# Layer 1's banded attention with TensorE's order written out by hand

## The chip, the cores and the metric
The kernel runs on one core of one Trainium2 chip. The metric is the device time of one launch in microseconds (us); lower is better.

## The reference
A two-layer encoder over one sequence of 2048 tokens of width 1024, in float32. Layer 0 mixes a dilated and a differential attention. Layer 1, which the change touches, is banded grouped-query attention: 16 query heads of 64, four to each of 4 key/value heads, each token attending to the 128 tokens on either side, with a learned sink per head:

```python
proj = h @ w_in                                   # odd_mixer; h is the normalised, modulated x
q, k, v, g = jnp.split(proj, [MIX_WIDTH, MIX_WIDTH + C_KV_WIDTH, MIX_WIDTH + 2 * C_KV_WIDTH], axis=-1)
...
m, l, acc = banded_attention(q, k, v, slopes, 1, C_HALF_WINDOW)
sk = sink.astype(jnp.float32).reshape(C_KV_HEADS, R)[None, :, :, None]
M = jnp.maximum(m, sk)
e = jnp.exp(m - M)
y = acc * e[..., None] / (l * e + jnp.exp(sk - M))[..., None]
y = y.transpose(0, 3, 1, 2, 4).reshape(B, S, MIX_WIDTH).astype(h.dtype)
return (y * jax.nn.silu(g)) @ w_out
```

## The kernel before
Tokens lie in 16 tiles of 128 and 4 blocks of 512 (TB = 4). TensorE is PE here, VectorE DVE, ScalarE ACT, GpSimd POOL; SP issues nearly all DMAs. Each float32 product is made of three matmuls on split operands (`three`, L292: high x high, high x low, low x high), so a 512-column step over one of 8 slices of the width is 3 matmuls, and a projection piece (128 columns of the weights for one block) is 24.

Layer 1 for a block b needs its normalised and transposed h (`layer1_norm`, eight tiles `pt_h` of four transposes, split into `h1T` by ACT, POOL and DVE), then `layer1_qkv`: two key pieces, one value piece (`pn`, 256 columns, weights `wh`/`wl`), eight query pieces. `layer1_gate` has eight gate pieces for a block. In `proj_pieces` the raw weights `wr` are loaded, ACT makes the high half of `wt` (L340), and DVE (even pieces) or POOL (odd pieces) the low half (L341); for the value piece POOL makes both low halves (L355). `wt`, `wh` and `wl` share two buffers. h of blocks 0, 1 and 2 is stored to `hD1` (L1068) and read again as `h1G` (L1090) for the gates.

`attend` (L1114) treats one tile t, for which keys and values of tiles t-1 to t+1 are loaded, and goes through four groups kv of four heads. A head's scores are `pqC` (L586, L587); DVE adds the distance table and takes the row maximum (L1146) into `sC` and `mxC`; one DVE multiply per group makes `nmC` (L1151); ACT takes the exponential (L1154). For each key tile u the four heads' scores are transposed into `ptC` (L1160), split into `hC` and `lC` (for u = t by ACT and POOL, else by ACT and DVE; L1166 to L1171) and multiplied with the values into `pyC` (L1173). The denominators of all 16 heads are made on DVE and ACT (L1184 to L1188), transposed on PE (`pd`, L1190), copied (`dtC`), stored to memory (`fC`, L1193), read back twice with broadcast (L1196), and POOL multiplies `yC` with them (L1198).

In the loop over blocks, attention of the tiles whose keys are there goes along with the projections of the next block, by a `tick` after each group; with block 3 go the gates of blocks 3, 0 and 1, and those of block 2 follow after attention, tied behind its last score. That is the order in which the code is written; the order on every engine is set by a scheduler that simulates the program (`schedule_with_timeline_sim=True`), so instructions may run elsewhere than where they are written. Each engine's queue is then fixed.

Of the kernel before, what the change touches and what calls it, by code (L numbers as in the profile page):

```python
# [11 lines left out]
F32 = mybir.dt.float32  # L12
# [9 lines left out]
P = 128  # L22
# [59 lines left out]
def tile_encoder(ctx: ExitStack, tc: tile.TileContext, x, c, ada_w, ada_b, norm_g, ab_w_in, ab_w_out,  # L82
# [7 lines left out]
    def scratch(name, shape, dt=F32):  # L90
        return dram.tile(shape, dt, name=name, tag=name)
# [9 lines left out]
    hD = scratch("hD", [TB, 2, P, KC * 512])  # L101
    hD1 = scratch("hD1", [TB - 1, 2, P, KC, 512])
    fB = scratch("fB", [B_H, S], F32)
# [227 lines left out]
    def proj_pieces(pool, ps, w, h, b, pieces, name, after=lambda b, n: None):  # L331
# [3 lines left out]
        for n, (c0, sink_T, sink_N) in enumerate(pieces):  # L335
            if sink_T is not None:
# [6 lines left out]
                for k in range(KC):  # L343
                    three(pt, (wt[:, 0, k], wt[:, 1, k]), (h[0][k], h[1][k]), k, KC, None if k else after(b, n))
                sink_T(pt, b)
                yield
            else:
# [8 lines left out]
                for j in range(4):  # L356
                    pt = ps.tile([P, 512], F32, name=f"pn_{name}_{b}_{n}_{j}", tag="mm")
                    cols = slice(j * P, (j + 1) * P)
                    for k in range(KC):
                        three(pt[:, :CH], (h[0][k][:, cols], h[1][k][:, cols]), (hi[:, k], lo[:, k]), k, KC)  # L360
                    sink_N(pt[:, :CH], 4 * b + j)
                    yield
# [328 lines left out]
    def dilated_attention(pool, poolc, ps_, fill, psf):  # L691
# [49 lines left out]
        def tick():  # L741
            steps[0] += 1
            if steps[0] % 2 == 0:
                next(gate, None)

# [308 lines left out]

    def layer1_norm(pool, ps, b):
# [7 lines left out]
        h = [[pool.tile([P, 512], FR, name=f"h1T{b}_{i}_{k}", tag="hk", bufs=20) for k in range(KC)] for i in range(2)]  # L1063
        norm_block(pool, ps, 1, b, xs, h)
        if b < TB - 1:
            for k in range(KC):
                for i in range(2):
                    nc.sync.dma_start(hD1[b, i, :, k], f32(h[i][k]))  # L1068
        return h

# [13 lines left out]
    def layer1_gate(pool, ps, h, b, after=lambda b, n: None):  # L1084
        if h is None:
            h = [[pool.tile([P, 512], FR, name=f"h1G{b}_{i}_{k}", tag="hk", bufs=20) for k in range(KC)]
                 for i in range(2)]
            for k in range(KC):
                for i in range(2):
                    nc.sync.dma_start(f32(h[i][k]), hD1[b, i, :, k])  # L1090
# [22 lines left out]

    def attend(pool, ps, t, V, consts, tick):  # L1114
        tab, nsl, isl, sk = consts
        u0, u1 = max(t - 1, 0), min(t + 2, NT)
        n, o = (u1 - u0) * P, (u0 - t + 1) * P
        for u in range(u0, u1):
# [13 lines left out]
        for a in range(2):  # L1132
            nc.sync.dma_start(f32(Q)[a * 64:(a + 1) * 64],
                              qC[t // 4][a, :, :, t % 4 * P:(t % 4 + 1) * P].rearrange("h f s -> f h s"))
# [4 lines left out]
        for kv in range(C_KV):  # L1139
            Sx = []  # L1140
            for r in range(4):
                h = 4 * kv + r
                pq = ps.tile([P, 384], F32, name=f"pqC{t}_{h}", tag="s")
                last = scores(pq[:, :n], Q[:, h], KH[:, kv, :n], Q[:, h], KL[:, kv, :n])
                s_ = pool.tile([P, 384], F32, name=f"sC{t}_{h}", tag="p", bufs=8)
                nc.vector.tensor_tensor_reduce(out=s_[:, :n], in0=pq[:, :n], in1=tab[:, o:o + n], scale=1.0,  # L1146
                                               scalar=isl[:, h:h + 1], op0=OP.add, op1=OP.max,
                                               accum_out=mx[:, h:h + 1])
                Sx.append(s_)
            hs = slice(4 * kv, 4 * kv + 4)  # L1150
            nc.vector.tensor_tensor(nm[:, hs], mx[:, hs], nsl[:, hs], op=OP.mult)  # L1151
            for r in range(4):
                h = 4 * kv + r
                nc.scalar.activation(Sx[r][:, :n], Sx[r][:, :n], AF.Exp, bias=nm[:, h:h + 1], scale=slope_C(h),  # L1154
                                     accum_out=ls[:, h:h + 1])
            py = ps.tile([P, 512], F32, name=f"pyC{t}_{kv}", tag="y")
            for u in range(u0, u1):
                pt = ps.tile([P, 512], F32, name=f"ptC{t}_{kv}_{u}", tag="t")
# [13 lines left out]
                for i, w in enumerate((hi, lo)):  # L1172
                    nc.tensor.matmul(py, V[u][:, kv], w, start=(u == u0 and i == 0), stop=(u == u1 - 1 and i == 1))  # L1173
            tmp = pool.tile([P, 512], F32, name=f"hsC{t}_{kv}", tag="hs", bufs=2)
            nc.scalar.activation(tmp[64:], py[64:], AF.Copy)
            for a in range(2):
                nc.vector.tensor_tensor(
                    y[a * 64:(a + 1) * 64, 2 * kv:2 * kv + 2],
                    tmp[64:].rearrange("p (g a q) -> p a g q", a=2, q=P)[:, a],
                    py[:64].rearrange("p (g a q) -> p a g q", a=2, q=P)[:, a], op=OP.add)  # L1180
            tick()

        d = sm.tile([P, C_H], F32, name=f"dC{t}", tag="dC", bufs=2)
        nc.vector.tensor_tensor(d, sk, nm, op=OP.add)  # L1184
        nc.scalar.activation(d, d, AF.Exp)
        nc.vector.tensor_tensor(d, d, ls, op=OP.add)
        nc.vector.tensor_scalar(d, d, 2.0, None, op0=OP.mult)
        nc.vector.reciprocal(d, d)  # L1188
        pd = ps.tile([P, 512], F32, name=f"pd{t}", tag="y")
        nc.tensor.transpose(pd[:C_H, :P], d, ident)  # L1190
        dt = sm.tile([C_H, P], F32, name=f"dtC{t}", tag="dtC", bufs=2)
        nc.scalar.activation(dt, pd[:C_H, :P], AF.Copy)
        nc.sync.dma_start(fC[t], dt)  # L1193
        F = pool.tile([P, KC, P], F32, name=f"fC_{t}", tag="f", bufs=1)
        for a in range(2):
            nc.sync.dma_start(F[a * 64:(a + 1) * 64].rearrange("p k q -> p (k q)"),  # L1196
                              fC[t].rearrange("(k a) q -> a k q", a=2)[a:a + 1].to_broadcast([64, KC, P]))
        nc.gpsimd.tensor_tensor(y, y, F, op=OP.mult)  # L1198
        nc.sync.dma_start(yC[t], y)
        return last  # L1200

# [12 lines left out]
    with sbuf("pO") as pool_:  # L1214
# [8 lines left out]
        with sbuf("pO2") as pool2, psum("psO") as ps_:  # L1223
# [9 lines left out]
            layer0_out(pool, Bufs(ps_, o=5), w, [upper, lower], g, x, x1d, "0", "o", range(FULL))  # L1233
            h1 = layer1_norm(pj, psj, 0)
            for _ in layer1_qkv(pj, psj, h1, 0, qs):
# [5 lines left out]
    with sbuf("pC") as pool, psum("psC") as ps_:  # L1241
        ps = Bufs(ps_, s=2, t=2, y=2)
        consts = layer1_consts(pool)
        V = {}
        for b in range(TB):
            ts = range(max(4 * b - 1, 0), 4 * b + 3 if b < TB - 1 else NT)

            if b + 1 < TB:
                h1 = layer1_norm(pj, psj, b + 1)
                between, n = layer1_qkv(pj, psj, h1, b + 1, qs), 14  # L1250
            else:
                between, n = chain(*(layer1_gate(pj, psj, h1 if g == TB - 1 else None, g)
                                     for g in (TB - 1, *range(TB - 2)))), 8 * (TB - 1)
            at = [0, 0]

            def tick():
                at[0] += 1
                while at[1] * len(ts) * C_KV < at[0] * n:
                    at[1] += 1
                    next(between, None)  # L1260

            for t in ts:
                last = attend(pool, ps, t, V, consts, tick)
            for _ in between:
# [42 lines left out]
```

## Time and profile before

| | |
|---|---|
| median of 3 runs | 3063.69 us (3059.81 to 3064.14) |
| the profiled execution, its span | 3054.52 us, 3052.5 us |
| mean granted TensorE clock | 0.964 |
| layer 0's last matmul starts | 2119.14 us |
| layer 1's last attention product starts | 2821.51 us |

Times in the profile count from the start of the span. The durations of matmuls overlap, since they are pipelined; the pace of PE is read from their starts. A wait is put down to the instruction whose result came last.

### The profile page before, as it was taken

The page shows a single profiled execution, that of the slowest core. Times are in us where ns is not written, and L with a number is a line of the kernel's source. Part 1 is how long each engine was busy: PE and PEld are TensorE (multiplying, and loading weights), DVE is VectorE, ACT ScalarE, POOL GpSimd, SP SyncE. Part 2 cuts the span into 40 slices and gives each one's busy share as a digit, 9 for nine tenths or more (in the row PEclk, how much of TensorE's full clock was granted, in tenths as well). Part 3 has the DMA queues.
Part 4 walks back from the last instruction along what each step waited for, and adds up shares of the span by engine and source line. Part 5 has one row for each costly group of instructions (what it writes and reads, how often), then busy time and mean ns, then how long its engine had stood idle before and what let it go on. Part 6 is the DMA issues. An engine that isn't in the chain of part 4 may idle for free. (4 is left out here: it accounts for less than half of the span.)

```text
span 3052.5 us, 43787 instructions
## 1 busy us (share of the span) xinstructions
PE 2797.3 (92%) x15056; PEld 2351.4 (77%) x15056; DVE 1894.7 (62%) x4120; ACT 1491.3 (49%) x2841; POOL 1147.5 (38%) x755
## 2 busy tenths in 40 slices
PE   6999899999999998899888887999889999999997
PEld 5788788878888887677776666787778788877786
DVE  7425286777677678755556767454465765556576
ACT  5311255556555555555556762223465765656321
POOL 3200075555655644322424333332334443333221
PEclk9999899999999999999999998999999999999999
DMA  6687743653655551298786888685988778885754
GB/s 264 228 289 232 208 139 109 190 176 121 165 157 161 153 167 42 64 273 238 201 238 172 203 226 246 222 295 198 246 205 223 188 179 205 228 214 154 219 187 155
DMA packets 554552, 593.78 MB, mean 195 GB/s; under 512 B 32257, under 2 KB 421594, under 8 KB 548186
## 3 DMA queue, kind: packets, MB, share of 16 engines
q1 hardware_dynamic: 542490, 574.21, 65.6%
q10 hardware_dynamic: 11840, 16.78, 1.6%
q8 instruction: 119, 1.95, 0.3%
q14 instruction: 103, 0.84, 0.1%
HBM read 414.36 MB, written 176.46 MB: 194 GB/s over the span
## 5 line engine op out<-in xcount | busy, mean ns | idle before, releaser
L637 ACT ACTIVATE s<-s,nm 128x2048 f32<-128x2048 f32 x128 | 256.7, 2006 | 140.5 <-DVE nm L636 140.4
L643 POOL TENSOR_SCALAR s<-s,rr 128x1536 f32<-128x1536 f32 x64 | 122.7, 1916 | 342.3 <-DVE rr L641 237.7
L586 PE MATMUL pq<-kB,q 128*128 128x512 f32 x512 | 217.5, 425 | 29.5 <-DVE mx L631 16.5
L646 POOL TENSOR_TENSOR s<-s,s 128x1536 f32<-128x1536 f32 x64 | 231.7, 3620 | 4.9
L658 ACT ACTIVATE th<-pt 128x512 fp32r<-128x512 f32 x256 | 147.1, 594 | 174.6 <-PE pt L654 132.3
L1146 DVE CUSTOM_DVE_ANT_0 sC<-pqC,tabC,isl 128x384 f32<-128x384 f32 (+1 forms) x256 | 147.5, 597 | 125.0 <-PE pqC L587 73.9
L587 PE MATMUL pq<-kB,q 128*128 128x512 f32 x512 | 206.7, 404 | 0.0
L631 DVE CUSTOM_DVE_ANT_0 s<-pq,ndist 128x1024 f32<-128x1024 f32 x128 | 156.0, 1218 | 78.1 <-PE pq L587 56.0
L659 DVE TENSOR_TENSOR tl<-pt,th 128x512 fp32r<-128x512 f32 x256 | 170.4, 683 | 51.0 <-ACT th L658 50.7
L631 DVE CUSTOM_DVE_ANT_0 s<-pq,ndist,mx 128x1024 f32<-128x1024 f32 x128 | 163.5, 1277 | 28.5 <-PE pq L587 26.0
L1154 ACT ACTIVATE sC<-sC,nmC 128x384 f32<-128x384 f32 (+1 forms) x256 | 151.0, 593 | 39.8 <-DVE nmC L1151 39.5
L297 PE MATMUL py<-tl,vB 128*128 128x256 f32 x512 | 152.4, 298 | 14.7 <-DVE tl L659 13.8
L654 PE MATMUL pt<-ident,s 128*128 128x128 f32 x1024 | 153.1, 277 | 2.7 <-DVE s L644 2.2
L294 PE MATMUL py<-th,vB 128*128 128x256 f32 x512 | 150.2, 293 | 2.4 <-ACT th L658 2.3
L586 PEld LDWEIGHTS pq<-kB,q 128*128 128x128 f32 x512 | 98.9, 193 | 62.9 <-DVE mx L631 26.0
L298 PE MATMUL py<-th,vB 128*128 128x256 f32 x512 | 146.3, 286 | 0.0
L341 POOL TENSOR_TENSOR wt_g<-wr_g,wt_g 128x1024 fp32r<-128x1024 f32 x32 | 77.1, 2408 | 182.8 <-ACT wt_g L340 177.5
L989 POOL TENSOR_TENSOR yr<-yr,gr 128x512 f32<-128x512 f32 (+1 forms) x46 | 62.5, 1360 | 209.5 <-DMA yr<-yC 37.2
L1167 POOL TENSOR_SCALAR hC<-rC 128x512 fp32r<-128x512 f32 x64 | 42.6, 666 | 255.9 <-ACT rC L1166 220.0
L1160 PE MATMUL ptC<-ident,sC 128*128 128x128 f32 x736 | 134.0, 282 | 3.1 <-ACT sC L1154 2.6
L294 PE MATMUL pp_l<-h1T,wt_l 128*128 128x512 f32 x320 | 129.0, 404 | 7.3 <-ACT wt_l L340 6.8
L298 PE MATMUL pp_l<-h1T,wt_l 128*128 128x512 f32 x320 | 129.0, 405 | 5.4 <-POOL wt_l L341 3.4
(417 smaller groups left out, 9181.7 us busy)
## 6 DMA issues: line engine op xcount, KB each, us to landing
wr_a<-in_ab_w_in_dram SPq DMA_DIRECT2D x48, 512.0 KB
wr_l<-in_c_w_in_dram SPq DMA_DIRECT2D x48, 512.0 KB
hD<-h0T SPq DMA_DIRECT2D x8, 2048.0 KB
aw_ss<-in_ada_w_dram SPq DMA_DIRECT2D x32, 512.0 KB
hs_a<-hD SPq DMA_DIRECT2D x16, 1024.0 KB
q<-qB SPq DMA_DIRECT2D x128, 128.0 KB
wr_g<-in_ab_w_in_dram SPq DMA_DIRECT2D x32, 512.0 KB
hs_g<-hD SPq DMA_DIRECT2D x16, 1024.0 KB
```

Source lines behind the costliest of these rows:

```text
L294: first = nc.tensor.matmul(pt, l[0], r[0], start=(k == 0), stop=False)
L297: nc.tensor.matmul(pt, l[0], r[1], start=False, stop=False)
L298: nc.tensor.matmul(pt, l[1], r[0], start=False, stop=(k == nk - 1))
L586: first = nc.tensor.matmul(ps_, q0, k0, start=True, stop=False)
L587: nc.tensor.matmul(ps_, q1, k1, start=False, stop=True)
L631: nc.vector.tensor_tensor_reduce(out=s_[:, half * 1024:(half + 1) * 1024], in0=pq, in1=ndist[:, o:o + 1024], scale=1.0, scalar=LOW if half ...
L637: nc.scalar.activation(s_, s_, AF.Exp, bias=nm, scale=slope_B(h), accum_out=lsum[:, a, t:t + 1])
L646: nc.gpsimd.tensor_tensor(Pm[0][:, W:], Pm[0][:, W:], Pm[1][:, W:], op=OP.add)
L654: nc.tensor.transpose(pt[:, kk, j], A[j][:, kb * P:(kb + 1) * P], ident)
L659: nc.vector.tensor_tensor(lo, src, f32(hi), op=OP.subtract)
L1146: nc.vector.tensor_tensor_reduce(out=s_[:, :n], in0=pq[:, :n], in1=tab[:, o:o + n], scale=1.0, scalar=isl[:, h:h + 1], op0=OP.add, op1=OP.max,
L1154: nc.scalar.activation(Sx[r][:, :n], Sx[r][:, :n], AF.Exp, bias=nm[:, h:h + 1], scale=slope_C(h), accum_out=ls[:, h:h + 1])
```

## The change
Within layer 1's attention the scheduler no longer orders PE: `manual_schedule` keeps PE's instructions in the order in which the code is written. The other engines are ordered as before. `attend` is split into a function that issues the loads and one that returns, for each group, three score parts (heads 0 and 1, head 2, head 3), three turns (the transposes and the split of one key tile) and three products. `parts_of` writes one group's three parts: scores of this group, then the product whose turn lay two parts back, then one turn of the group before, then as many projection steps as an even rate asks for. One step is now one slice of the width (3 matmuls; 6 in the value piece), where it was a piece. `nmC` is made three times per group. Gates of blocks 1 and 2 now go along with the projections of the blocks after them, from `h1T` as it lies there; with block 3 go the gates of block 3 and five of block 0's eight pieces, and three pieces are left for after attention. So only block 0's h is stored to `hD1` and read again: 16 stores and 16 loads where there were 48 and 48. In layer 0 the gate's steps are counted so that nothing moves.

```diff
+            if k < KC - 1:          # proj_pieces: yields after each slice of the width
+                yield
...
-    def attend(pool, ps, t, V, consts, tick):
+    def load_attend(pool, t, V, parts=1):
...
+        def group(kv):
+            Sx, parts, py = {}, {}, []
+            def score(rs):
...
+            def turn(u):
...
+            def product(u):
...
+            return ([partial(score, rs) for rs in ((0, 1), (2,), (3,))],
+                    [partial(turn, u0 + i) for i in range(3)], [partial(product, u0 + i) for i in range(3)])
...
+        with tc.manual_schedule(engines={nc.tensor.engine}):
+            tiles = {0: load_attend(pool, 0, V)}
+            before, pend = [], []
+            def parts_of(step, filling, rate):
+                for j in range(3):
+                    if step:
+                        step[0][j]()
+                    if len(pend) >= 2:
+                        pend.pop(0)()
+                    if before:
+                        before[0][1][j]()
+                        pend.append(before[0][2][j])
+                    at[0] += rate
+                    while at[1] + 1 <= at[0]:
+                        at[1] += 1
+                        next(filling, None)
+                before[:] = [step] if step else []
...
+                if 0 < b < TB - 1:
+                    fills, n = [layer1_gate(pj, psj, h1, b)], 64
+                if b + 1 < TB:
+                    h2, xs = [[], []], layer1_norm(pj, b + 1)
+                    fills += [layer1_h(pj, psj, b + 1, xs, h2, False), layer1_qkv(pj, psj, h2, b + 1, qs)]
+                    n += 8 + 96
+                else:
+                    rest = layer1_gate(pj, psj, None, 0)
+                    fills, n = [layer1_gate(pj, psj, h1, b), rest], 64 + 40
+                filling, at = chain(*fills), [0, 0]
+                rate = n / (3 * C_KV * len(ts))
+                for t in ts:
+                    for kv, step in enumerate(attend(pool, ps, t, V, consts, tiles[t])):
+                        parts_of(step, filling, rate)
+                        if kv == 1 and t + 1 < ts.stop:
+                            tiles[t + 1] = load_attend(pool, t + 1, V)
...
+            for _ in filling:
+                pass
...
-        for _ in layer1_gate(pj, psj, None, TB - 2, lambda b, n: last):
-            pass
```

How this moves instructions shows at three places. The first is PE where layer 0's output projection (`po0c`) ends. Before, the transposes of block 1's normalised x (`pt_h_1`) follow:

```order
L298 MATMUL po0c_1_20483<-woh0a,yl0c_0_20523 128x512
L265 MATMUL pt_h_1_0_20668<-ident,x_4_20612 128x128
L265 MATMUL pt_h_1_0_20668<-ident,x_5_20614 128x128
L265 MATMUL pt_h_1_0_20668<-ident,x_6_20616 128x128
L265 MATMUL pt_h_1_0_20668<-ident,x_7_20618 128x128
L265 MATMUL pt_h_1_1_20677<-ident,x_4_20612 128x128
```

Scores of layer 1 (`pqC`) first come 123 rows further down. After the change the same place reads:

```order
L298 MATMUL po0c_1_20483<-woh0a,yl0c_0_20523 128x512
L590 MATMUL pqC_0_20671<-khC_20618,qC_20620 128x256
L591 MATMUL pqC_0_20671<-klC_20619,qC_20620 128x256
L590 MATMUL pqC_1_20676<-khC_20618,qC_20620 128x256
L591 MATMUL pqC_1_20676<-klC_20619,qC_20620 128x256
L265 MATMUL pt_h_1_0_20686<-ident,x_4_20627 128x128
L265 MATMUL pt_h_1_0_20686<-ident,x_5_20629 128x128
L265 MATMUL pt_h_1_0_20686<-ident,x_6_20631 128x128
L265 MATMUL pt_h_1_0_20686<-ident,x_7_20633 128x128
L265 MATMUL pt_h_1_1_20697<-ident,x_4_20627 128x128
```

The scores of tile 0's heads 0 and 1 now stand ahead of block 1's transposes, which came first before.

The second place is PE where block 2's value projection begins (`pn_l_2_2_0`, weights `wh_l_2_2` and `wl_l_2_2`), behind key piece 1 (`pp_l_2_1`). Before, its first matmul has rows of attention between, and its second comes later still:

```order
L294 MATMUL pp_l_2_1_22407<-h1T_0_7_22120,wt_l_2_1_22404 128x512
L297 MATMUL pp_l_2_1_22407<-h1T_1_7_22128,wt_l_2_1_22404 128x512
L298 MATMUL pp_l_2_1_22407<-h1T_0_7_22120,wt_l_2_1_22404 128x512
...
L586 MATMUL pqC_12_22542<-khC_22219,qC_22221 128x384
L587 MATMUL pqC_12_22542<-klC_22220,qC_22221 128x384
L586 MATMUL pqC_13_22547<-khC_22219,qC_22221 128x384
L587 MATMUL pqC_13_22547<-klC_22220,qC_22221 128x384
L294 MATMUL pn_l_2_2_0_22513<-wh_l_2_2_22503,h1T_0_0_22113 128x256
L1173 MATMUL pyC_1_22362<-lC_1_3_22380,vC_21638 128x512
```

Five rows of attention are left out here, so nine lie between the two in all. After the change:

```order
L1186 MATMUL ptC_3_4_23154<-ident,sC_15_23070 128x128
L294 MATMUL pp_l_2_1_23091<-h1T_7_False,wt_l_2_1_23088 128x512
L297 MATMUL pp_l_2_1_23091<-h1T_7_True,wt_l_2_1_23088 128x512
L298 MATMUL pp_l_2_1_23091<-h1T_7_False,wt_l_2_1_23088 128x512
L294 MATMUL pn_l_2_2_0_23184<-wh_l_2_2_23174,h1T_0_False 128x256
L297 MATMUL pn_l_2_2_0_23184<-wl_l_2_2_23175,h1T_0_False 128x256
```

The value projection now follows the piece directly, and its second matmul, the first to read `wl`, comes at once.

The third is POOL's queue in block 1's tiles around a multiplication with the divisors (the rows `yC`). Before, around tile 4's:

```order
L341 TENSOR_TENSOR wt_l_2_7_23426<-wr_l_2_7_23424,wt_l_2_7_23426 128x1024
L1167 TENSOR_SCALAR hC_3_4_23002<-rC_3_23004 128x512
L1168 TENSOR_TENSOR lC_3_4_23003<-rC_3_23004,hC_3_4_23002 128x512
L341 TENSOR_TENSOR wt_l_2_9_23659<-wr_l_2_9_23657,wt_l_2_9_23659 128x1024
L1198 TENSOR_TENSOR yC_22670<-yC_22670,fC_23036 128x1024
L1167 TENSOR_SCALAR hC_0_5_23098<-rC_0_23100 128x512
L1168 TENSOR_TENSOR lC_0_5_23099<-rC_0_23100,hC_0_5_23098 128x512
L1167 TENSOR_SCALAR hC_1_5_23199<-rC_1_23201 128x512
```

Weights of the projections (`wt_l`) stand ahead of `yC` and splits of the next tile behind it. After the change, from tile 4's `yC` on:

```order
L1241 TENSOR_TENSOR yC_22573<-yC_22573,fC_23322 128x1024
L341 TENSOR_TENSOR wt_l_2_3_23404<-wr_l_2_3_23402,wt_l_2_3_23404 128x1024
L1193 TENSOR_SCALAR hC_1_5_23473<-rC_1_23475 128x512
L1194 TENSOR_TENSOR lC_1_5_23474<-rC_1_23475,hC_1_5_23473 128x512
L341 TENSOR_TENSOR wt_l_2_5_23602<-wr_l_2_5_23600,wt_l_2_5_23602 128x1024
```

The low half of query piece 3's weights, `wt_l_2_3`, now stands behind tile 4's `yC`, and the next tile's `lC_1` behind both. PE after the change, from tile 4's `pd` to the readers of these, 48 rows of attention and value projection being left out:

```order
L1206 MATMUL pyC_3_23210<-lC_3_5_23219,vC_22325 128x512
L1233 MATMUL pd_23317<-ident,dC_23311 16x128
L1186 MATMUL ptC_0_5_23327<-ident,sC_0_23111 128x128
...
L298 MATMUL pn_l_2_2_3_23354<-wh_l_2_2_23174,h1T_7_True 128x256
L294 MATMUL pp_l_2_3_23407<-h1T_0_False,wt_l_2_3_23404 128x512
L297 MATMUL pp_l_2_3_23407<-h1T_0_True,wt_l_2_3_23404 128x512
L298 MATMUL pp_l_2_3_23407<-h1T_0_False,wt_l_2_3_23404 128x512
L590 MATMUL pqC_8_23422<-khC_22811,qC_22813 128x384
L591 MATMUL pqC_8_23422<-klC_22812,qC_22813 128x384
L590 MATMUL pqC_9_23427<-khC_22811,qC_22813 128x384
```

The first matmul that reads the low half of `wt_l_2_3` (L298) now stands 50 rows behind `pd`.

## Rows read from the trace of the kernel before

**Rows 1.** The page: busy time by engine, with the share of the span.
```profile
PE 2797.3 (92%) x15056; PEld 2351.4 (77%) x15056; DVE 1894.7 (62%) x4120; ACT 1491.3 (49%) x2841; POOL 1147.5 (38%) x755
```

**Rows 2.** By window: us; busy PE, PEld, DVE, ACT, POOL (xcount); PEclk, DMA share, GB/s.
```profile
2119.00:2145.00 26.00, 22.76 (x119) 18.35 (x118) 10.49 (x47) 9.40 (x13) 11.43 (x11) 0.93 0.88 265
2145.00:2825.00 680.00, 634.01 (x3278) 525.71 (x3277) 412.83 (x1033) 414.95 (x952) 257.48 (x195) 0.96 0.81 204
2250.00:2450.00 200.00, 184.35 (x973) 151.30 (x973) 135.81 (x346) 135.13 (x306) 93.16 (x74) 0.94 0.82 210
2560.00:2780.00 220.00, 212.64 (x1080) 177.74 (x1078) 127.71 (x313) 131.46 (x296) 77.48 (x56) 0.99 0.83 213
```

**Rows 3.** Waits of PE, 2145 to 2825 us, first of 13: total us, times, longest us.
```profile
PE pqC L586 <- DVE mxC L1146: 6.9, 9, 2.4
```

**Rows 4.** Timeline of PE at the end of layer 0: start us, us, line, out<-in.
```profile
2118.91 0.39 PE L297 MATMUL po0c<-wol0a,yh0c 128*128 128x512 f32 x1
2119.14 0.39 PE L298 MATMUL po0c<-woh0a,yl0c 128*128 128x512 f32 x1
2119.37 1.03 PE L265 MATMUL pt_h<-ident,x 128*128 128x128 f32 x8
```

**Rows 5.** Gate pieces on PE, 2119 to 2825 us: xcount | busy, mean ns | idle before.
```profile
L297 PE MATMUL pp_g<-h1G,wt_g 128*128 128x512 f32 x155 | 62.7, 404 | 5.1 <-DMA h1G<-hD 5.1
...
L294 PE MATMUL pp_g<-h1T,wt_g 128*128 128x512 f32 x64 | 25.6, 401 | 0.0
```

**Rows 6.** Timeline: the last store of x on SP, the first score on PE.
```profile
2121.02 0.33 SPq L1034 DMA_DIRECT2D x1d<-xo0c  x1
...
2149.43 0.55 PE L586 MATMUL pqC<-khC,qC 128*128 128x256 f32 x1 [3.39 <-issue]
```

**Rows 7.** Groups of POOL and ACT, 2119 to 2825 us.
```profile
L1168 POOL TENSOR_TENSOR lC<-rC,hC 128x512 fp32r<-128x512 f32 x64 | 84.0, 1313 | 4.9
...
L1198 POOL TENSOR_TENSOR yC<-yC,fC 128x1024 f32<-128x1024 f32 x15 | 36.0, 2401 | 59.6 <-DMA fC<-fC 45.3 <-DVE mxC L1146 6.2 <-PE pqC L587 4.8
L341 POOL TENSOR_TENSOR wt_l<-wr_l,wt_l 128x1024 fp32r<-128x1024 f32 x14 | 34.4, 2456 | 56.6 <-ACT wt_l L340 56.6
...
L271 ACT ACTIVATE hr<-pt_h,AB 128x512 f32<-128x512 f32 x24 | 17.8, 777 | 14.4 <-PE pt_h L265 12.6 <-DVE h1T L273 1.6
```

**Rows 8.** Timeline of PE around its wait before the value projection.
```profile
2139.18 0.58 PE L294 MATMUL pn_l<-wh_l,h1T 128*128 128x256 f32 x1 [1.77 <-DVE lo_kc L371]
...
2142.34 0.36 PE L297 MATMUL pn_l<-wl_l,h1T 128*128 128x256 f32 x1
2142.54 0.28 PE L298 MATMUL pn_l<-wh_l,h1T 128*128 128x256 f32 x1
2142.66 0.28 PE L294 MATMUL pn_l<-wh_l,h1T 128*128 128x256 f32 x1
```

**Rows 9.** Timeline: pd on PE and yC on POOL, tiles 10 and 14.
```profile
2626.36 0.27 PE L1190 MATMUL pd<-ident,dC 128*16 128x128 f32 x1
...
2642.76 2.38 POOL L1198 TENSOR_TENSOR yC<-yC,fC 128x1024 f32<-128x1024 f32 x1 [9.20 <-DMA fC<-fC]
...
2791.33 0.41 PE L1190 MATMUL pd<-ident,dC 128*16 128x128 f32 x1
...
2798.38 2.38 POOL L1198 TENSOR_TENSOR yC<-yC,fC 128x1024 f32<-128x1024 f32 x1 [0.75 <-DMA fC<-fC]
```

**Rows 10.** DMA: bytes of 2145 to 2825 us.
```profile
DMA packets 162679, 138.94 MB, mean 204 GB/s; under 512 B 6772, under 2 KB 137012, under 8 KB 162627
```

**Rows 11.** DVE: nm, the line L1151: min/median/max ns.
```profile
L1151 DVE TENSOR_TENSOR nmC<-mxC,nsl x64: 149/164/1696, 2155.7 to 2803.4; 128x4 f32<-128x4 f32 x64
```

**Rows 12.** Timeline around the end of attention: PE, SP, PE.
```profile
2821.51 0.40 PE L1173 MATMUL pyC<-lC,vC 128*128 128x512 f32 x1
...
2841.53 0.92 SPq L962 DMA_DIRECT2D wor1b<-in_c_w_out_dram  x2
...
2853.92 0.39 PE L294 MATMUL po<-woh1b,yh 128*128 128x512 f32 x1
```

More of the change, by code (lines that the diff above doesn't have):

```diff
@@ L743, in tick @@
             if steps[0] % 2 == 0:
-                next(gate, None)
+                for _ in range(KC):
+                    next(gate, None)
         for hp in range(A_H // 2):
@@ L1062, in layer1_norm, with layer1_h @@
         norm_rows(pool, 1, b, xs)
[L1063 to L1066, printed above, removed]
+        return xs
+    def layer1_h(pool, ps, b, xs, h, keep):
+        for k in range(KC):
+            for part in h:
+                part.append(pool.tile([P, 512], FR, name=f"h1T{b}_{len(part)}_{part is h[1]}", tag="hk", bufs=20))
+            pt = ps.tile([P, 512], F32, name=f"pt_h1_{b}_{k}", tag="t")
+            transposed(pt, xs, k)
+            modulate(pool, 1, f"{b}_{k}", pt, k, (h[0][k], h[1][k]))
+            if keep:
                 for i in range(2):
-                    nc.sync.dma_start(hD1[b, i, :, k], f32(h[i][k]))
-        return h
+                    nc.sync.dma_start(hD1[i, :, k], f32(h[i][k]))
+            yield
     def layer1_qkv(pool, ps, h, b, qs):
@@ L1138, in attend @@
         y = pool.tile([P, KC, P], F32, name=f"yC_{t}", tag="y", bufs=2)
[L1139 to L1157, printed above, removed]
@@ new lines, in group @@
+        def group(kv):
+            Sx, parts, py = {}, {}, []
+            def score(rs):
+                for r in rs:
+                    h = 4 * kv + r
+                    pq = ps.tile([P, 384], F32, name=f"pqC{t}_{h}", tag="s")
+                    scores(pq[:, :n], Q[:, h], KH[:, kv, :n], Q[:, h], KL[:, kv, :n])
+                    Sx[r] = pool.tile([P, 384], F32, name=f"sC{t}_{h}", tag="p", bufs=8)
+                    nc.vector.tensor_tensor_reduce(out=Sx[r][:, :n], in0=pq[:, :n], in1=tab[:, o:o + n], scale=1.0,
+                                                   scalar=isl[:, h:h + 1], op0=OP.add, op1=OP.max,
+                                                   accum_out=mx[:, h:h + 1])
+                hs = slice(4 * kv + rs[0], 4 * kv + rs[-1] + 1)
+                nc.vector.tensor_tensor(nm[:, hs], mx[:, hs], nsl[:, hs], op=OP.mult)
+                for r in rs:
+                    h = 4 * kv + r
+                    nc.scalar.activation(Sx[r][:, :n], Sx[r][:, :n], AF.Exp, bias=nm[:, h:h + 1], scale=slope_C(h),
+                                         accum_out=ls[:, h:h + 1])
+            def turn(u):
+                if u >= u1:
+                    return
@@ L1171, in attend @@
                     nc.vector.tensor_tensor(lo, pt, f32(hi), op=OP.subtract)
[L1172 to L1175, printed above, removed]
-            for a in range(2):
[L1177 to L1180, printed above, removed]
@@ L1192, in attend @@
[L1192 to L1200, printed above, removed]
+                parts[u] = hi, lo
@@ new lines, in product @@
+            def product(u):
+                if u >= u1:
+                    return
+                if u == u0:
+                    py.append(ps.tile([P, 512], F32, name=f"pyC{t}_{kv}", tag="y"))
+                for i, w in enumerate(parts[u]):
+                    last = nc.tensor.matmul(py[0], V[u][:, kv], w, start=(u == u0 and i == 0),
+                                            stop=(u == u1 - 1 and i == 1))
+                if u < u1 - 1:
+                    return
+                tmp = pool.tile([P, 512], F32, name=f"hsC{t}_{kv}", tag="hs", bufs=2)
+                nc.scalar.activation(tmp[64:], py[0][64:], AF.Copy)
+                for a in range(2):
+                    nc.vector.tensor_tensor(
+                        y[a * 64:(a + 1) * 64, 2 * kv:2 * kv + 2],
+                        tmp[64:].rearrange("p (g a q) -> p a g q", a=2, q=P)[:, a],
+                        py[0][:64].rearrange("p (g a q) -> p a g q", a=2, q=P)[:, a], op=OP.add)
+                if kv == C_KV - 1:
+                    end()
+                return last
@@ L1203, in tile_encoder @@
+        return [group(kv) for kv in range(C_KV)]
     with_G, with_A, with_AC = ExitStack(), ExitStack(), ExitStack()
@@ L1244, in tile_encoder @@
         V = {}
[L1245 to L1264, printed above, removed]
+        with tc.manual_schedule(engines={nc.tensor.engine}):
[15 more added lines that the diff above has]
+                before[:] = [step] if step else []
+            for b in range(TB):
+                ts = range(max(4 * b - 1, 0), 4 * b + 3 if b < TB - 1 else NT)
+                fills, n = [], 0
+                if 0 < b < TB - 1:
[14 more added lines that the diff above has]
+                            tiles[t + 1] = load_attend(pool, t + 1, V)
+                if b + 1 < TB:
+                    for _ in filling:
+                        pass
+                    h1 = h2
+                    tiles[ts.stop] = load_attend(pool, ts.stop, V, C_KV)
+            parts_of(None, filling, 0)
+            while pend:
+                pend.pop(0)()
+            for _ in filling:
```

54 lines of the change are left out of this document (35 added, 19 removed).

## The prediction

> **What bounds the kernel now.** The page comes first: TensorE (PE) is busy for 92% of the span and no other engine passes 62%, so the question is what PE loses, and where [rows 1]. The view by windows puts layer 1's attention at 2145 to 2825 us: PE shows 634 us of work in 680, at a mean granted clock of 0.96, while DVE, ACT and POOL are busy for 413, 415 and 257 us and DMA for 0.81 of the time [rows 2]. No second engine is the bound there; PE waits for results.
>
> **What the change can win** is this: 46 us of idle time between 2145 and 2825, 0.04 x 680 = 27 us by the clock, and before 2145, from layer 0's end, 3 idle and 2 by the clock: 78 us. It is spread unevenly. From 2250 to 2450 us the stage loses 15.7 idle and 12 by clock of 200 us (14%), from 2560 to 2780 us 7.4 and 2.2 of 220 (4.4%) [rows 2]. In the list of PE's waits the largest entry is 6.9 us in nine pieces: many small waits, and no single one to remove [rows 3].
>
> **The change part by part.** The matmuls are the same, so the sum has three kinds of terms: these 78 us go, new losses come, and work changes places. Durations on PE overlap, so the pace is read from starts: 0.227 us for 512 columns, 0.109 for a transpose (eight in 1.03 us) [rows 4], 0.12 for 256 columns [rows 8]; I take 0.17 for 384, three quarters of the first.
>
> *Work moved.* By 2825 us the kernel before has done 155 + 64 three-matmul steps of its gates, of 256 [rows 5]; about 5 of them stand behind the last product at 2821.51 [rows 12]. So 42 steps are left there; the new order leaves 24. That puts 18 x 3 x 0.227 = 12.3 us more work ahead of the last product.
>
> *Start.* Layer 0's last matmul starts at 2119.14. Before, PE goes straight on with transposes of block 1 [rows 4] and its first projections, and needs tile 0's queries only at 2149.43, after standing 3.39 us [rows 6]. The new order puts the scores of heads 0 and 1 first. SP issues attention's loads behind the last store of x, at 2121.02. The stores of h that lay among these loads are gone; what is left ahead of the scores is x 0.5 MB, V 0.5, K 1.0 and queries 1.0: 3 MB at the 265 GB/s of this stretch [rows 2] are 11.5 us, with up to three for issue. The queries land at 2132 to 2136, so PE stands 12 to 17 us; I take 15. The work that needs only x now lies behind it. This term is new and sure in sign.
>
> *h of a block.* Each of eight transposed tiles is read by 0.78 us of ACT for 0.44 of PE [rows 7, 4]; standing together they wait up to 8 x 0.34 = 2.7 us a block. Three blocks, some of it lost today too: 4 (0 to 8).
>
> *Value projection.* Its weights take the buffers that the piece ahead of it frees, and it now follows that piece directly. POOL's half is like the 2.46 us of wt_l [rows 7]. Where that happened before, PE waited 1.77 us [rows 8]; with a pair of lC work (1.31 and its copy) ahead on POOL it is about 4. I take 2.5 for block 1 and 4 each for blocks 2 and 3: 10.5 (5 to 14). Piece 3 behind it wants two conversions in a row: 3 us in block 1.
>
> *The divisors' round trip.* Each of 16 tiles sends 1/d through memory: pd on PE, a copy, a store, two loads, then POOL multiplies (yC, 2.40 us). POOL works in order and stood 45 us for these loads [rows 7]. From pd to yC the trace shows 7.0 us at the shortest and 16.4 at the longest [rows 9]. PE pays little for it today, because scores and projections run ahead of what stands behind yC. In a written order they cannot. Counting the new order at the paces above, PE wants what stands behind yC this long after pd: weights of piece 3, 6.5 us (tiles 4 and 8; ready 4.8 after yC starts); weights of piece 9, 13.3 (tiles 5 and 9; 4.8); lC of the next tile 16.5 (tiles 3 and 7; 8.0), 17 to 19 in the rest of blocks 0 to 2, but 13.0 for tiles 10 to 13 and 10.2 for tile 14, where there is less filling (4.3; tile 11 6.7); the last gate weights 11.6 (4.8). With 7 us from pd to yC only pieces 3 and tiles 11, 14 and 15 stall, 2 x 5.3 + 2 = 12.6 us together; with 9 us it is 26, with 11 us 50. I take 9, nearer the short end, because two of three blocks of h, 16.8 of 139 MB, no longer pass through DMA [rows 10]; and of the 26 a quarter is taken off, since other waits in between give POOL time: 20 (8 to 45).
>
> The Trainium skill, page DMA: Bandwidth & Descriptors, section Anatomy of one DMA, gives a transfer about 2 us of fixed cost, most of it the receipt of the last byte. By it the two transfers of this trip would take 4 us (an estimate), the term would be near 6, and the time about 3055. The rows do not bear that out here: the shortest trip took 7.0 us.
>
> *Parts.* The 128 more nm multiplies take 0.16 us each [rows 11], 20 us of DVE, which is free for 40% of the stage; if that cover is gone they cost up to 20. Head 3's score is turned one part later, 3.3 us of PE work in block 3; I take nothing for it (0 to 8). The wait of 5.1 us for re-read h [rows 5] is inside the 78.
>
> *Clock.* After the wait of 1.77 us matmuls start 0.20 us apart until 2142.54, then 0.12: half clock for 3.4 us, 1.7 lost [rows 8]. Of the waits above about 13 are that long: 22 (14 to 30).
>
> The new losses are 15 + 4 + 10.5 + 3 + 20 + 22 = 74.5 against 78; with 12.3 of work moved the last product comes 9 us later, at about 2830. *The tail* does not give the moved work back: today gates fill PE from 2821.51 until the first matmul with the second third of the output weights at 2853.92; these weights are issued on SP 20 us behind the last product [rows 12]. In the new SP order they stand behind the last gate piece's store, about as late, and PE, with less filling, stands. I give 2 us back (0 to 12). That makes +7 us on the profiled execution's 3054.5, 3061.5. The median of the runs lies 9 us above that execution, so the forecast is 3070.
>
> **Rivals.** *Evenness wins.* The whole stage loses no more than 2560 to 2780 us, 4.4% of some 640, 28 us, beside the start (15), value projections (10.5), piece 3 (3) and h (4): 60, 18 less than today. With 12 moved and up to 12 given back the time falls by 6 to 18; with 14 it is 3050. For it: no engine is near full, and trips of up to 16.4 us lie in that window. Against: it holds no value projection, and its order could go around POOL. It decides if pd to yC falls to 7 us.
>
> *POOL's wait becomes PE's.* With 11 us from pd to yC the term is 45, and four more dips of the clock cost 7: +32, so 3102. For it: 11 is still short of the middle of the trace's extremes; against: fewer transfers.
>
> *The clock does not settle.* If PE waits as in [rows 8] in every other one of the 64 groups, 32 x 1.7 = 54 us go by the clock instead of 22: 3102 again. Against it: 2250 to 2450 us, the worst stretch, still has 0.94 [rows 2]. The Trainium skill, page TensorE: Matmul & The Clock Gate, section A second HAM failure mode, tells of a kernel in which frequent short idle times between groups of matmuls made the clock swing so; this trace shows part of it.
>
> *Nothing to be seen.* Old and new losses agree to within 6 us: 3064. My sum lies 6 from this.
>
> **How the numbers follow.** The measurement tells about 0.2%, 6 us, from no change. The forecast (trips of 8 to 10.5 us) has 0.40 and ends between -6 and +20 us, so that a third of it lies within 6; evenness has 0.32, nearly all of it faster; the two dear cases 0.22; no change 0.06. Faster 0.34, same 0.22, slower 0.44. The range reaches from below the first rival, with losses at the low ends of h, clock and value projection (3034), to the dear rivals (3100); the likeliest case alone holds 3057 to 3084.
>
> **What the new profile would show.** PE standing until about 2134 before its first score; waits of pp_l for POOL's wt_l of 5 to 8 us in blocks 2 and 3; waits of pyC for lC after tiles 10 to 14; a value projection that waits for POOL's wl; no wait for re-read h; a clock near 0.96; the last product near 2830. I am wrong if trips take 7 us, if the queries land before 2128, or if PE's idle time outside the start falls below 35 us.

## The result

The changed kernel takes 3099.54 us (median of 4 runs, 3094.59 to 3107.2) against 3061.75 us before (3051.74 to 3064.14): a ratio of 1.0132, 95% interval 1.0099 to 1.0165, 38 us slower. A second set of runs gave 1.0100 (1.0076 to 1.0124), 28 us. The direction was forecast, the size was not: the forecast, 3070, lay 6 us above the kernel before, and the stated range, up to 3100, just holds the first set.

**The profile after.** The page shows PE busy for slightly less of a longer span [rows 1]:

```profile
span 3092.8 us, 43719 instructions
...
PE 2791.0 (90%) x15056; PEld 2353.0 (76%) x15056; DVE 1949.1 (63%) x4248; ACT 1494.0 (48%) x2841; POOL 1147.1 (37%) x755
```

Layer 0's last matmul starts at 2122.04 and the last attention product at 2863.00: 741.0 us between them, 702.4 before [rows 4, 12]. From there to the end it is 229.8 us, 231.0 before. So the whole loss, 38.6 us, lies in the stretch that was rewritten. The windows of that stretch (us; busy PE, PEld, DVE, ACT, POOL; clock, DMA share, GB/s), whole and in three parts:

```profile
2122.04:2863.00 740.96, 655.88 (x3433) 551.47 (x3431) 480.10 (x1210) 429.46 (x966) 271.11 (x206) 0.95 0.71 176
...
2240.20:2328.80 88.60, 88.60 (x451) 74.68 (x450) 65.81 (x161) 58.61 (x130) 35.61 (x25) 1.00 0.81 198
...
2333.00:2440.00 107.00, 92.69 (x503) 79.02 (x502) 62.77 (x147) 57.10 (x125) 40.30 (x31) 0.94 0.65 175
2684.90:2863.00 178.10, 154.64 (x778) 127.28 (x776) 118.17 (x320) 109.00 (x263) 64.85 (x51) 0.93 0.64 154
```

Idle time is 85 us. But look at the second row, from tile 1's pd to tile 3's: PE has no listed wait there, and the written order keeps it busy for all of 88.6 us at full clock. The divisors of tile 1 take 12.2 us from pd to yC in it, which costs nothing, since what stands behind yC is wanted later than that. The kernel before, between the same two pd:

```profile
2238.07:2316.18 78.11, 69.20 (x377) 56.83 (x376) 53.95 (x139) 52.65 (x122) 36.71 (x31) 0.91 0.86 240
```

The new order is dense where nothing is late, and pays at a few places. PE's waits name them, from 2122 to 2863 us (total us, times, longest):

```profile
PE pqC L590 <- DMA qC<-qC: 20.5, 1, 20.5
PE pp_l L298 <- POOL wt_l L341: 18.4, 6, 6.1
PE pyC L1206 <- POOL hC L1193: 14.5, 5, 7.6
PE pn_l L297 <- POOL wl_l L357: 9.7, 5, 2.4
PE pyC L1206 <- POOL lC L1194: 6.0, 8, 1.7
PE pt_h L265 <- DVE gg_g L412: 3.9, 2, 1.9
PE pt_h L265 <- ACT hr L271: 3.5, 7, 1.3
PE pp_l L294 <- ACT wt_l L340: 2.4, 3, 1.1
PE pp_l L294 <- ACT hr L271: 2.2, 2, 1.1
```

Five entries hold 69 of the 85 us; the small waits of before, led by 6.9 us in nine pieces [rows 3], are nearly gone. The costliest wait on POOL in single rows (start, length, engine, line; in brackets the idle time before and who ended it), tile 11:

```profile
2721.92 0.27 PE L1233 MATMUL pd<-ident,dC 128*16 128x128 f32 x1
...
2732.07 1.27 SPq L1239 DMA_DIRECT2D fC<-fC  x2
...
2737.33 2.34 POOL L1241 TENSOR_TENSOR yC<-yC,fC 128x1024 f32<-128x1024 f32 x1 [10.87 <-DMA fC<-fC]
2739.63 2.34 POOL L341 TENSOR_TENSOR wt_g<-wr_g,wt_g 128x1024 fp32r<-128x1024 f32 x1
2741.94 0.62 POOL L1193 TENSOR_SCALAR hC<-rC 128x512 fp32r<-128x512 f32 x1
...
2742.61 0.80 PE L1206 MATMUL pyC<-hC,vC 128*128 128x512 f32 x1 [7.64 <-POOL hC L1193]
...
2746.68 0.63 PE L294 MATMUL pp_g<-h1T_False,wt_g 128*128 128x512 f32 x1
2747.11 0.63 PE L297 MATMUL pp_g<-h1T_True,wt_g 128*128 128x512 f32 x1
```

POOL stands 10.87 us for the divisors, multiplies, converts gate weights that PE first reads 10 us after the conversion, at 2751.74, and only then splits the scores that PE is waiting for. Behind the wait matmuls of 512 columns start 0.43 us apart, where 0.23 is their full pace: the clock is at the lower of its two levels, 1.2 of 2.4 GHz.

### The profile page after: what moved, and what is told of

Its sections match the earlier page's. It is cut to its first block, busy times and chain, and to the rows that moved or that the text cites. A ratio compares the mean times of both kernels' runs of the same rounds, so it can differ in the third digit from the quotient of the medians.

```text
span 3092.8 us, 43719 instructions
## 1 busy us (share of the span) xinstructions
PE 2791.0 (90%) x15056; PEld 2353.0 (76%) x15056; DVE 1949.1 (63%) x4248; ACT 1494.0 (48%) x2841; POOL 1147.1 (37%) x755
## 5 line engine op out<-in xcount | busy, mean ns | idle before, releaser
L650 POOL TENSOR_TENSOR s<-s,s 128x1536 f32<-128x1536 f32 x64 | 229.8, 3590 | 4.9
L297 PE MATMUL py<-tl,vB 128*128 128x256 f32 x512 | 152.8, 298 | 13.9 <-DVE tl L663 13.2
L298 PE MATMUL py<-th,vB 128*128 128x256 f32 x512 | 146.5, 286 | 0.0
L298 PE MATMUL pp_l<-h1T_False,wt_l 128*128 128x512 f32 x320 | 127.4, 399 | 18.4 <-POOL wt_l L341 18.4
L294 PE MATMUL pp_l<-h1T_False,wt_l 128*128 128x512 f32 x320 | 133.1, 416 | 4.6 <-ACT wt_l L340 2.4
L1196 ACT ACTIVATE hC<-ptC 128x512 fp32r<-128x512 f32 x120 | 71.3, 594 | 132.9 <-PE ptC L1186 131.8
```

The costliest lines, as they stand in the source:

```text
L294: first = nc.tensor.matmul(pt, l[0], r[0], start=(k == 0), stop=False)
L297: nc.tensor.matmul(pt, l[0], r[1], start=False, stop=False)
L298: nc.tensor.matmul(pt, l[1], r[0], start=False, stop=(k == nk - 1))
L650: nc.gpsimd.tensor_tensor(Pm[0][:, W:], Pm[0][:, W:], Pm[1][:, W:], op=OP.add)
```

## The experiments

A trace gives the stretch from layer 0's last matmul to the last product ("stretch" below); for the kernel before it is 702.4 us, for the changed one 741.0 and, in its second set, 732.6. Ratios are to the kernel before in the same set of runs, where its median lay between 3055.8 and 3061.8 us; so kernels of different sets are compared by their ratios. One trace is one execution, and stretches of the same kernel differ by 8 us here.

**Scores later at the start.**

```diff
+                if b == 0:
+                    for _ in range(24):
+                        next(filling)
+                    n -= 24
                 rate = n / (3 * C_KV * len(ts))
```

> The changed kernel, with 24 filling steps (block 1's eight transposed tiles and its two key pieces) written ahead of tile 0's first scores. Theory A (the new losses are places where the written order puts a waiting instruction ahead of work that is ready): PE's wait of 20.5 us for the queries falls under 4 us, and the run takes 16 to 20 us less than the changed kernel, about 3081. Rival B (the even order is full, so a wait that is removed comes back at the next place): at most 6 us less. Both expect the waits behind POOL's yC to stay.

Measured: 3089.97 us, 1.0118 (1.0097 to 1.0140), between the two sets of the changed kernel, 1.0132 and 1.0100; the stretch, 736.6, lies between theirs too. PE's wait for the queries fell from 20.5 to 3.3 us, but no gain shows: B. The 143 us from the first score on, here and in the changed kernel:

```profile
2146.60:2290.00 143.40, 131.58 (x693) 112.20 (x694) 97.22 (x256) 86.60 (x205) 49.80 (x38) 0.94 0.81 204
```

```profile
2142.90:2286.00 143.10, 135.56 (x734) 115.62 (x735) 97.69 (x252) 90.08 (x205) 53.51 (x42) 0.97 0.82 200
```

With 24 of 104 steps taken out of it, the filling of block 0's groups is too thin: idle time goes from 7.5 to 11.8 us and the clock from 0.97 to 0.94. Of the 17 us that the start won, tile 2's pd, counted from layer 0's last matmul, shows 7.0 against the changed kernel and 4.2 against its second set. PE's waits for wt_l, hC and lC were also dearer in this trace, 43.4 us against 38.9 and 35.2.

**POOL without the multiplication.** Left out: `nc.gpsimd.tensor_tensor(y, y, F, op=OP.mult)`, and nothing else.

> The changed kernel without POOL's multiplication of y by the inverse divisors (this part of the computation is left out; the trip of the divisors through memory stays). Theory A: PE's waits for POOL's wt_l (18.4 us), hC (14.5) and lC (6.0) fall from 39 to under 10 us in all, with some ten half-clock dips of 1.7 us gone too: 35 to 48 us less, about 3057. Rival B: POOL's share moves on to ACT and DVE, at most 15 us less. Rival C (block 3 waits because its filling is thin, not because of POOL's queue): waits in block 3, 22 us, stay, 15 to 20 us less.

Measured: 3052.25 us, 0.9989 (0.9972 to 1.0005), 1.4% below the changed kernel's ratio, 44 us (34 by its second set); stretch 698.7. Waits for wt_l are 5.1 us, for lC 3.0, for hC none. That is A, and not thin filling: block 3 is as thinly filled here and waits 5.6 us, where it waited 23.4.

**The scheduler's order on the changed program.** `with ExitStack():` in place of `with tc.manual_schedule(...)`.

> The changed kernel with PE's order left to the scheduler again, all else as changed (parts, moved gates, fewer stores of h). Theory A: the start's wait and most of the waits behind yC go, some 17 us of short gaps come back: 30 to 45 us less, about the time of before, 3055 to 3070. Rival C (the gates moved ahead and the thin filling of block 3 cost the time): 3085 or more.

Measured: 3041.57 us, 0.9957 (0.9944 to 0.9971): less than A said, and 13 us faster than the kernel before. The stretch is 703.1 us with 128 more matmuls in it than before:

```profile
2118.27:2821.35 703.08, 667.80 (x3506) 557.59 (x3504) 487.34 (x1213) 434.23 (x971) 269.49 (x208) 0.98 0.76 187
```

The rest of the change (smaller steps, gates along with the block they belong to, two blocks of h not stored and read again) is thus a gain as a whole, its parts not tested one by one; the written order alone loses it and 30 to 40 us more. Rival C falls.

**POOL's multiplication later.** Nothing left out; PE's order is the same, row for row. On the other engines, which the scheduler orders anew, about 90 of 9800 rows change place.

```diff
+            def divide():
+                m = nc.gpsimd.tensor_tensor(y, y, F, op=OP.mult)
+                if t < NT - 1:                       # split_lo: the latest lC on POOL
+                    tc.add_manual_dep(m.ins, split_lo[0].ins.name, ORDER, reason="behind the next tile's split")
+                nc.sync.dma_start(yC[t], y)
+            tails.append(divide)                     # called after the next tile's group 2
```

> The changed kernel with one edit: POOL's yC of tile t is ordered behind the lC of the next tile's second group, some 13 to 18 us after pd, so that what stood behind yC no longer waits for the trip; PE's order is the same, nothing is left out. Theory A: as without the multiplication, less a few us for yC itself: 30 to 45 us less, about 3062. Rival B: at most 15 us less, since other splits then wait behind yC.

Measured: 3059.39 us, 1.0015 (0.9999 to 1.0030), 36 us below the changed kernel's ratio (26 by its second set); stretch 707.9. The waits that are left, 2118 to 2826 us:

```profile
PE pqC L590 <- DMA qC<-qC: 20.0, 1, 20.0
PE pn_l L297 <- POOL wl_l L357: 9.6, 5, 2.4
PE pp_l L294 <- ACT hr L271: 6.5, 2, 3.2
PE pp_l L298 <- POOL wt_l L341: 5.1, 3, 1.7
...
PE pyC L1208 <- POOL lC L1196: 3.1, 5, 0.8
```

Of 38.9 us behind POOL's yC 8.2 are left, and POOL stands for the divisors in two late tiles of 16 only, 13.2 us in all. A again; the first two entries are the next places.

**Both.** The two edits together.

> Both earlier edits together: POOL's yC behind the next tile's second split, and 24 steps of block 1's h and keys ahead of the first scores, which leaves fewer steps to fill block 0's groups. The first edit alone gave about 38 us, the second alone 7, since the first tiles lost again what the start won. Theory A (the start's gain was eaten by tiles that were left with too little filling): against the kernel with the first edit alone 5 to 8 us less, 3052. Theory A' (it was eaten by longer trips of the divisors, which by chance took 0.5 us more): 12 to 16 us less, 3045.

Measured: 3050.71 us, 0.9979 (0.9960 to 0.9998), 9 to 11 us less than with the late yC alone; stretch 701.4. That lies between A and A'. Tile 2's pd comes 10.6 us earlier in the stretch than with the late yC alone, for some 14 us of work moved to the front, so part of it is missed as filling behind the start. That longer trips ate the rest in the run without the late yC is not shown: the trips took 10.65 us on the mean there, against 10.50 and 10.18 in the two traces of the changed kernel.

**Gates of block 0 at the start.**

```diff
+                if b == 0:
+                    for _ in layer1_gate(pj, psj, h1, 0, range(3)):
+                        pass
...
-                    rest = layer1_gate(pj, psj, None, 0)
-                    fills, n = [layer1_gate(pj, psj, h1, b), rest], 64 + 40
+                    rest = layer1_gate(pj, psj, None, 0, range(3, 8))
+                    fills, n = [layer1_gate(pj, psj, h1, b), rest], 64 + 16
```

> POOL's yC behind the next tile's second split, and three gate pieces of block 0 (24 steps, read from its h as it lies there) ahead of the first scores instead of in block 3, where 16 steps of block 0's gates are left; 24 stay for the tail as before. The other blocks keep their filling. Theory A: the 20 us of standing at the start turn into 16.4 us of work, and block 3 gets shorter by as much, since its waits were POOL's and not those of thin filling: 15 to 18 us less than with the first edit alone, about 3042. Rival C (block 3 needs its filling): 0 to 8 us less, and waits of 5 us or more on ACT or DVE in block 3.

Measured: 3049.38 us, 0.9976 (0.9960 to 0.9991), 10 us less, between A and rival C; stretch 701.6. The wait at the start is 3.5 us. But the last 200 us before the last product lose 11.5 idle now, against 6.5 with the late yC alone (us; busy PE, ...):

```profile
2623.00:2823.00 200.00, 188.45 (x985) 153.02 (x983) 163.75 (x405) 139.69 (x330) 78.51 (x63) 1.00 0.75 185
```

```profile
2626.00:2826.00 200.00, 193.54 (x1023) 161.59 (x1021) 156.92 (x401) 139.69 (x327) 79.85 (x63) 1.00 0.76 189
```

With four steps a group instead of five PE comes to each product a little before its split is ready, in waits below 1.2 us. Filling in block 3 is needed too, though less than rival C had it.

**Conversions on DVE.** In layer 1, piece 3's low half and the first half of the value piece's.

```diff
-                (nc.gpsimd if n % 2 else nc.vector).tensor_tensor(wt[:, 1], ...
+                (nc.gpsimd if n % 2 and (name, n) != ("l1", 3) else nc.vector).tensor_tensor(wt[:, 1], ...
-                    nc.gpsimd.tensor_tensor(lo[:, ks], wr, f32(hi[:, ks]), op=OP.subtract)
+                    (nc.gpsimd if i or name != "l1" else nc.vector).tensor_tensor(lo[:, ks], wr, ...
```

> POOL's yC behind the next tile's second split, and in layer 1 the low half of piece 3's weights, and of the first half of the value piece's, made by DVE (1.2 us) instead of POOL (2.4 us). Theory A: the waits for wl (9.6 us) and for piece 3's wt fall by half, with a dip of the clock or two: 6 to 10 us less than with the first edit alone, about 3051. Rival: DVE's own queue is fuller in these places, no gain or a loss of up to 4 us.

Measured: 3052.02 us, 0.9988 (0.9967 to 1.0010), 7 us less by the medians, as A said, though the interval overlaps that of the late yC alone; stretch 703.5. The mechanism held in half only. PE's waits for piece 3's wt_l fell from 5.1 to 1.6 us, but those for wl only from 9.6 to 8.2. In blocks 2 and 3 DVE's conversion starts 0.26 us behind POOL's of the other half and takes 3.17 us; in block 1 it starts first and takes 1.23, and POOL's takes 3.44 in place of 2.34:

```profile
2167.41 1.23 DVE L357 TENSOR_TENSOR wl_l<-wr_l,wh_l 128x1024 fp32r<-128x1024 f32 x1 [0.47 <-PE pp_l L298]
2167.46 3.44 POOL L357 TENSOR_TENSOR wl_l<-wr_l,wh_l 128x1024 fp32r<-128x1024 f32 x1 [2.48 <-PE pp_l L298]
...
2365.03 2.34 POOL L357 TENSOR_TENSOR wl_l<-wr_l,wh_l 128x1024 fp32r<-128x1024 f32 x1 [8.27 <-ACT rC L1194]
2365.29 3.17 DVE L357 TENSOR_TENSOR wl_l<-wr_l,wh_l 128x1024 fp32r<-128x1024 f32 x1
```

So the two engines did not convert side by side in these pairs: the one that started later took 1.1 and 1.9 us longer than alone, about what was left of the other's conversion (1.2 and 2.1).

**All four.** The last three edits and, for blocks 1 and 2, a generator that takes one step of the last gate piece and one transposed tile in turn.

> The three edits (yC late, three gate pieces at the start, conversions on DVE) and a fourth: in blocks 1 and 2 the last gate piece's steps alternate with the next block's eight transposed tiles, which stood together. Theory A: the gains add up, 15 to 18 by the start, 6 to 10 by the conversions, 6 to 9 by the transposes: about 3028, faster than the kernel before by 0.9%, and than the scheduler's order of the changed kernel. Rival B (waits come back elsewhere): 3045 or more.

Measured: 3040.31 us, 0.9948 (0.9926 to 0.9969); stretch 686.7. Faster than the kernel before, and 19 us less than with the late yC alone, not the 31 that 3028 asked for: between A and B. The start had given 10 alone, not 15 to 18, and the conversions 7, with the same 8.2 us of waits for wl as here. That leaves 2 us for the transposes by the medians, where 6 to 9 were expected, but 10 by the stretches of single traces; PE's waits around the transposes (for hr, and for DVE behind a gate) are 11.2 us, 14.6 with the conversions alone. What the fourth edit gave stays open.

**The changed kernel again.**

> The changed kernel once more, beside the others of this call, so that differences of 10 us are taken on one chip. All theories: 1.0 to 1.6% above the kernel before, and a trip of the divisors of 10 to 11 us on average.

Measured: 3086.60 us, 1.0100 (1.0076 to 1.0124); stretch 732.6, waits in the same places (18.8 for the queries, 17.4 for wt_l, 11.6 for hC).

**More gates behind attention.** `64 + 16` steps along with block 3 instead of `64 + 40`, with the late yC.

> POOL's yC behind the next tile's second split, and 24 gate steps fewer along with block 3: 48 steps, 6 pieces, are left for after attention, about as many as before the change. Theory A (PE stands behind attention for the second third of the output weights, which are issued on SP some 20 us after the last product whatever PE does): the last product comes 7 to 16 us earlier, the 10 us wait in the tail is filled, in all 7 to 10 us less than with the late yC alone, 3050. Rival C (block 3 needs its filling): the last product comes at most 5 us earlier and nothing is won. Rival D (the weights wait for the last gate piece): the tail's wait stays as it is, 0 to 4 us less or more.

Measured: 3066.46 us, 1.0032 (1.0019 to 1.0046), about 5 us more than with the late yC alone, whose interval it meets; stretch 700.1. Rival D is the nearest. SP's rows in the tail (start, length):

```profile
2855.28 0.32 SPq L413 DMA_DIRECT2D G<-gg_g  x1
2860.76 1.41 SPq L967 DMA_DIRECT2D wor1b<-in_c_w_out_dram  x3
```

and in the changed kernel:

```profile
2884.18 0.32 SPq L413 DMA_DIRECT2D G<-gg_g  x1
...
2892.83 1.41 SPq L967 DMA_DIRECT2D wor1b<-in_c_w_out_dram  x3
```

These rows start 38 and 43 us behind the last product with more gates in the tail, 21 and 30 in the changed kernel. The weights follow the last gate piece, so pieces left to the tail do not fill the wait for them: it is 8.6 us where it was 10.8. And the stretch is shorter by 8 us, not by the 16.4 of 24 steps, since block 3's filling is thinner.

**All four, with more gates behind attention** (40 steps).

> The kernel of all four edits, with the 16 steps of block 0's gates that went along with block 3 left for after attention: 40 steps there. Theory A: the tail's wait of 11 us is filled, and block 3's groups, now with 3.2 steps each, lose some 3 to 6 us more to the splits: 3 to 8 us less than with all four edits, about 3035. Rival C: block 3 loses as much as the tail wins, no difference.

Measured: 3039.61 us, 0.9941 (0.9918 to 0.9964); stretch 681.6. No difference from all four that the intervals show: C.

**The scheduler with the late yC and DVE's conversions.**

> The changed kernel with yC late and the conversions on DVE, but with PE's order left to the scheduler. Theory A (the scheduler goes around these waits by itself): within 6 us of the run with the scheduler alone, about 3040. Rival (the same places hold the scheduler's order up too): 10 us or more below it, 3031.

Measured: 3033.23 us, 0.9923 (0.9897 to 0.9949), 0.8% faster than the kernel before and the best median here; its interval meets that of the scheduler alone, so whether these places hold the scheduler up as well stays open.

## Why the prediction was right in sign and wrong in size

The sum stood against the profiled execution; there the new span is 40.3 us longer, of which 2.9 lie in layer 0, where PE's order did not change.

*Start:* "I take 15", 12 to 17. It was 20.5. The 3 MB came at less than the 265 GB/s assumed: tile 1's loads were issued right behind tile 0's, and the window from 2122 to 2150 us moved 185 GB/s at a DMA share of 0.96:

```profile
2122.00:2150.00 28.00, 6.41 (x34) 5.13 (x33) 6.47 (x48) 4.99 (x11) 3.09 (x4) 0.63 0.96 185
```

The 265 belonged to another mix: with the stores of h in it a packet held 1270 bytes on the mean (2119 to 2152 us), here 966. Whether that is the cause was not tested.

*h of a block:* 4 forecast; waits of pt_h and of pp_l for hr and for DVE behind a gate are 9.6. *Value projection:* 10.5 forecast, 9.7 measured.

*The divisors' round trip:* **here the sum failed most.** With piece 3 the term was 23; PE's waits for wt_l, hC and lC measured 38.9. The mechanism, the tiles and the formula were right: tile 11 took 15.4 us from pd to yC, so lC's pair would be ready at 15.4 + 6.7 = 22.1 against 13.0, a stall of 9.1; measured 7.64 + 0.55. Tile 4 (8.5 us): 8.5 + 4.8 - 6.5 = 6.8; measured 6.1. The step that failed is "I take 9, nearer the short end". The trips took 7.8 to 15.4 us, 10.5 on the mean of 16 pairs of pd and yC (10.2 in the second set). The choice was made between the two extremes of the trace before, 7.0 and 16.4; its 16 pairs have a mean of 11.5, which that trace could have told. The reason given, fewer bytes, was too weak for the step from 11.5 to 9: in the stretch 130.7 MB moved in place of 145.0, the DMA share fell from 0.81 to 0.71, and the mean trip was shorter by 1 us. The quarter taken off for other waits did hold: with each tile's measured trip the formula gives 42 us, three quarters of it some 31, and 31 of the 38.9 us go when the multiplication is left out. The other 8, for POOL's wt_l and lC, do not hang on the trip; 3 of them, piece 3, were in the sum. With the clock and all that follows, the late yC is worth 33 us of the stretch (25 against the second set), the multiplication 42 (34).

*Clock:* 22 forecast. The mean of 0.95 over 741 us looks like 37, but much of that is lost while PE stands, where it costs nothing: in the wait for the queries PE did no work at all, and the granted clock was 0.60.

```profile
2122.43:2142.89 20.46, 0.00 (x0) 0.03 (x1) 2.74 (x37) 0.00 (x0) 0.00 (x0) 0.60 0.91 182
...
2340.30:2346.00 5.70, 5.45 (x29) 4.67 (x30) 4.02 (x7) 5.15 (x10) 5.42 (x5) 0.70 0.65 229
2370.60:2376.00 5.40, 4.18 (x30) 3.85 (x31) 0.79 (x3) 0.39 (x1) 4.10 (x3) 1.00 1.17 272
```

The trace's clock records give 34 us lost in the stretch, 15 of them inside PE's waits; before, 26 and 2.5. So outside waits the clock cost 19 us where it had cost 23 (15 in the second set): 22 was near. The step behind it, a dip (a few us at the lower clock) for every wait as long as that of [rows 8], did not hold. Of eleven waits of 1.7 to 2.5 us in this stretch five came with the lower clock, as the wait of 1.94 us before 2340.30 did (second row), and six did not, as that of 2.42 us before 2370.60 (third row).

*Added up:* new losses were forecast as 74.5 us and came to 104 (85 of waits, 19 by the clock). Of the 29.5 more, 16 are POOL's waits with piece 3, 5.5 the start, 5.6 h of a block and 6.3 small waits for ACT and DVE that the sum had not; the value projection and the clock gave back some 4. What was to go, 78, was 72 by the same count (49 and 23). With 12.3 us of work ahead of the last product that makes some 44 us, and the stretch grew by 38.6. The last 5 or 6 us are probably gaps too short to be listed, of which there are fewer now; nothing here measures them.

*Work moved and tail:* right. The tail gave back 1.2 us, 2 were forecast, and the weights do stand behind the last gate's store.

The *POOL* rival, priced 3102 at 11 us from pd to yC, comes nearest, in part by luck. It put the trips at 45, with a tenth off the 50 and not a quarter as in the forecast; 31 came, and the start, h and small waits made up for the rest. *Evenness* was right for tiles without a wait and wrong as a whole. *The clock does not settle* did not come: 19 us outside waits, not 54. Of the three signs of being wrong none came, since the miss lay on the other side: PE's waits outside the start were 65 us, where the terms of the sum made 37.5.

## What to carry to other kernels

An order written by hand is as good as the latest instruction in it: before it is fixed, ask of each engine's in-order queue what waits for memory there, and what stands behind it. Here one multiplication on POOL that nothing urgent needed held up splits and weights, and moving it won back most of the loss without touching PE's order. The length of such a wait is to be taken from all of its instances in the trace, not from its extremes. Filling that is moved to cover one wait is missed where it came from.

## What was not expected

Scheduled by its simulation, the changed program beats both kernels (0.9957) with yC not moved by hand: PE waits 11.2 us for wt_l, hC and lC there (2.1, 1.9 and 7.2), not 38.9, although the trips are longer, 8.2 to 17.0 us and 11.2 on the mean. So the price lies in what stands behind the trip and when it is wanted, not in its length alone. Fewer bytes shortened this chain of small transfers by little: 10% less in the stretch, and trips of 10.5 us on the mean, 11.5 before. With the late yC alone the stretch still carries 20 us of standing at the start, and yet the kernel is level with the one before.
